# Feed-forward stages of a two-layer decoder: VectorE's and ScalarE's queues in the order of the text, with silu placed behind a weight cast

## The chip, the core and the metric

The kernel runs on one core of a Trainium2 chip. Times are device microseconds (us) of one execution. The median of three runs before the change is 2691.31 us (2690.03 to 2691.76). Engines are named as in the profile: PE is TensorE's matmul, PEld its weight load, DVE is VectorE, ACT is ScalarE, POOL is GpSimd, SP is SyncE, which here issues the loads of the weights.

## What is computed

Two decoder layers over 256 tokens of width 2048: first a dilated-window attention, then a latent attention, each followed by a SwiGLU feed-forward. The change touches the feed-forward stages alone:

```python
D_MODEL = 2048; SEQ = 256; FFN_HIDDEN = 5632

def swiglu(xn, w_gu, w_down):
    g, u = jnp.split(xn @ w_gu, 2, axis=-1)
    return (jax.nn.silu(g) * u) @ w_down

...
        h = h + swiglu(rms_norm(h, ffn_norm_g[layer]), ffn_w_gu[layer], ffn_w_down[layer])
    return rms_norm(h, final_norm_g)
```

All of it is float32. The kernel multiplies in a reduced format (fp32r) and splits every number into a high and a low half, so that one product becomes three matmuls: high by high, high by low, low by high.

## The kernel before, in words

**Weights.** All weight matrices stream through one `WeightStream`, in a fixed list of units, here called weight tiles: 128 partitions by 2048 floats, 1 MB. A weight tile is loaded by SP into one of three `raw` buffers (two DMAs of 512 KB in the feed-forward), then split: ACT casts it to the high half `hi` (line 167 for a whole tile, line 157 for half of one), DVE subtracts to get the low half `lo` (line 168 or 158). There are three buffers each for `hi` and `lo`. `ws.next()` (line 196) hands out the next tile, and before that splits the tile two ahead and issues loads three ahead of that (`more`, line 192). So while PE works on tile k, tile k+2 is being split, into the buffers that tile k-1 has just left.

**Two kinds of tile.** An "eight" tile takes 24 matmuls of 512 columns. A "seven" tile (`SEVEN`, tiles 2, 4 and 6 of a group) saves one of eight block products: `split_blocks` first makes sums of its blocks on DVE (lines 181 to 183, into `raw` and `sums`), casts and subtracts the tile (`hi`, `lo`) and the sums (`th`, `tl`, one buffer each), and takes 21 matmuls. For it the activations need sums as well (`sums`, from line 656: `f` in line 661, four `g` in line 666, then two casts and two subtracts, into x itself and into `forms` or `forms_h`).

**Groups.** `mixed` computes one group: 8 weight tiles against x, into two accumulators of two PSUM banks each, `la` and `ra`, plus four single banks for the "seven" tiles. After the last "seven" tile the four banks are folded into two SBUF tiles, `left` and `right` (line 724 on ACT, lines 725 to 727 on DVE). In the last tile of a group the 12 matmuls of `la` come first, then the 12 of `ra`. When `la` is done, `close(0, la)` is called, then `ws.more()`, which splits the next group's tile 1; when `ra` is done, `close(1, ra)`. There are only two accumulators, so the next group's first matmul needs `la` to be read out.

**A gate/up group.** 512 hidden columns of gate and up. `close` (from line 745) adds the accumulator to `gate` or `up` (line 748, DVE), then either silu of both token tiles (line 752, ACT) or the product of up and silu (line 754, DVE). Afterwards `turned` is put off by one tile (`later.put(1, turned)`): it runs behind the first tile of what follows, and transposes the result on PE (line 405, eight transposes), splits it into `hT` (line 380 on ACT, line 381 on DVE), and for the groups j = 4, 8 and 12 of the first two parts also makes sums of `hT`. In the first group of a layer there is no "seven" tile: silu reads `la` itself, and the scalings of x (`scaled`, line 674) and its sums are put off into this group and the next one.

**Parts.** The 44 hidden tiles of 128 go in parts of 16, 16 and 12 (`FFN_PARTS`): four, four and three gate/up groups, each part followed by its down product. The down product of the first two parts is two `mixed` groups whose `close` adds to the residual `h` (line 770), after which POOL adds the folded part by accumulating DMAs (line 774). The down product of the last part goes by `product` and adds in line 778. There are 11 gate/up groups in a layer, 22 in all.

**What sets the order.** The text is a plain list of operations; every wait is derived from what the operations read and write. The order in each engine's queue is set by a planner when the program is built: it goes through its own reckoning of time and may move an instruction of an engine ahead of others that stand before it in the text, as long as its data are ready. Each engine then issues its queue in that order.

Of the kernel before, what the change touches and what calls it, by code (L numbers as in the profile page):

```python
# [13 lines left out]
AF = mybir.ActivationFunctionType  # L14
ALU = mybir.AluOpType
# [4 lines left out]
NT = S // P  # L20
# [25 lines left out]


SEVEN = (2, 4, 6)
SEVEN_DOWN = {16: (2, 4, 6), 12: ()}


# [173 lines left out]
def kernel(ctx, tc, consts, x, attn_norm_g, ffn_norm_g, a_w_qkv, a_w_o, kv_norm_g,  # L225
                       b_w_kv_a, b_kv_a_norm_g, b_w_kv_b, b_w_q_a, b_q_a_norm_g, b_w_q_b, b_w_o,
                       ffn_w_gu, ffn_w_down, final_norm_g, out):
    nc = tc.nc
# [95 lines left out]
    def units_ffn(layer):  # L324
        for k0, n in FFN_PARTS:
            v = ffn_w_gu[layer].rearrange("(k p) c -> p k c", p=P)
            for j in range(k0, k0 + n, 4):
                for kp in range(KD // 2):
                    blocks = [v[:, 2 * kp:2 * kp + 2, b + j * P:b + j * P + 512] for b in (0, FF)]
                    units.append((blocks, None, "seven" if j > 0 and kp in SEVEN else "eight"))  # L330
            v = ffn_w_down[layer].rearrange("(k p) c -> p k c", p=P)
# [212 lines left out]
    with tc.tile_pool(name="attn_a", bufs=2) as ap:  # L544
# [45 lines left out]
        for quad in range(HEADS // 4):  # L590
            vs = []
            for g in range(NG):
                acc = product(x_stationary, xT, KD)
# [4 lines left out]
            for pair in range(2):  # L598
                st = {}
                for g in range(NG):  # L600
                    qk = []
                    for which in range(2):
                        acc = product(w_stationary, xT, KD, cols=(col(0), col(1)))
                        t = ap.tile([P, 2, S], F32, tag=f"qk{which}", name=f"qk{which}")
# [34 lines left out]

    def ffn(xT, rstd, finish):  # L640

        with tc.tile_pool(name="ffn", bufs=1) as fp:
            ws.sum_pool = fp

            r2, rem = [small.tile([P, NT], F32, tag=m, name=m) for m in ("r2", "rem")]
# [5 lines left out]
            later.put(1, lambda: row.update(R=across(r2, "R")))  # L651
            forms = fp.tile([P, len(SEVEN), 2, 3, P], F32R, name="forms")

# [16 lines left out]
            def scaled(kp):  # L670
# [4 lines left out]
                if kp in SEVEN:  # L675
                    sums(xT, kp, forms[:, SEVEN.index(kp)])

            def mixed(X, pairs, seven, sums_of, left, right, close):

                la, ra = acc_tile(), acc_tile()
                pb, begun = None, set()

                def first(m):
                    new = m not in begun
                    begun.add(m)
                    return new

                def mul(out, x, w, i, st, sp):
                    (xh, xl), (wh, wl) = x, [t[:, i * 512:(i + 1) * 512] for t in w]
                    mm(out=out, lhsT=xh, rhs=wh, start=st, stop=False)  # L693
                    mm(out=out, lhsT=xh, rhs=wl, start=False, stop=False)  # L694
                    mm(out=out, lhsT=xl, rhs=wh, start=False, stop=sp)  # L695

                for kp in range(pairs):
                    ends = kp == pairs - 1
                    w = ws.next(late=ends)
                    x = lambda t, kk: [X[:, 2 * kp + kk, o + t * P:o + (t + 1) * P] for o in (0, S)]  # L700
                    if kp in seven:
                        i = seven.index(kp)
                        st, sp = i == 0, i == len(seven) - 1
                        if st:
                            pb = [bank() for _ in range(4)]
                        y = lambda j: x(1, 0) if j == 0 else [sums_of[:, i, h, j - 1, :] for h in range(2)]
                        mul(pb[0], x(0, 0), w[:2], 1, st, sp)
                        mul(la[:, 0], x(0, 1), w[:2], 3, first("la0"), False)
                        mul(pb[1], y(0), w[:2], 0, st, sp)
                        mul(ra[:, 0], y(3), w[:2], 2, first("ra0"), False)  # L710
                        mul(pb[3], y(2), w[2:], 0, st, sp)
                        mul(pb[2], y(1), w[2:], 1, st, sp)
                        mul(la[:, 1], x(1, 1), w[2:], 2, first("la1"), False)
                    else:
                        for i, (acc, m) in enumerate(((la, "la"), (ra, "ra"))):
                            for t in range(NT):
                                mul(acc[:, t], x(t, 0), w, 1 - i, first(f"{m}{t}"), False)
                                mul(acc[:, t], x(t, 1), w, 3 - i, False, ends)
                            if ends and i == 0:
                                close(0, la)  # L720
                                ws.more()
                    later.tick()
                    if seven and kp == seven[-1]:
                        nc.scalar.copy(out=left[:, 0], in_=pb[0])
                        nc.vector.tensor_tensor(out=left[:, 1], in0=pb[2], in1=left[:, 0], op=ALU.add)
                        nc.vector.tensor_tensor(out=left[:, 2], in0=pb[3], in1=left[:, 1], op=ALU.add)
                        nc.vector.tensor_tensor(out=right, in0=pb[1].unsqueeze(1).broadcast_to([P, NT, 512]),
                                                in1=left[:, 1:3], op=ALU.subtract)
                close(1, ra)
# [4 lines left out]
            for part, (k0, n) in enumerate(FFN_PARTS):  # L734
                last = part == len(FFN_PARTS) - 1
                hT = big_tile([P, 16, 2 * S], F32R, "hT")
                for j in range(0, n, 4):
                    gate, up = pair_tiles()
                    first = k0 + j == 0
                    if first:  # L740
                        for kp in range(KD // 2):
                            later.put(kp + 3, lambda kp=kp: scaled(kp))
                    sc_ = rstd if first else rem

                    def close(i, acc, first=first, both=(gate[:, 0:3:2], up), sc_=sc_):
                        d = both[i]
                        if not first:
                            nc.vector.tensor_tensor(out=d, in0=acc, in1=d, op=ALU.add)  # L748
                            acc = d
                        for t in range(NT):  # L750
                            if i == 0:
                                nc.scalar.activation(out=d[:, t], in_=acc[:, t], func=AF.Silu, scale=sc_[:, t:t + 1])
                            else:
                                nc.vector.scalar_tensor_tensor(out=d[:, t], in0=acc[:, t], scalar=sc_[:, t:t + 1],
                                                               in1=both[0][:, t], op0=ALU.mult, op1=ALU.mult)

                    def turned(j=j, up=up, hT=hT, seven=SEVEN_DOWN[n]):
                        transposed([up[:, t, :] for t in range(NT)], hT, j, None)
                        for kp in (j // 2, j // 2 + 1):
                            if kp in seven:  # L760
                                sums(hT, kp, forms_h[:, seven.index(kp)])
                    mixed(xT, KD // 2, () if first else SEVEN, forms, gate, up, close)
                    later.put(1, turned)

                for c in range(0, 0 if last else 4, 2):
                    left, right = pair_tiles()

                    def close(i, acc, c=c):
                        d = h[:, :, (c + i) * 512:(c + i + 1) * 512]
                        nc.vector.tensor_tensor(out=d, in0=acc, in1=d, op=ALU.add)  # L770

                    mixed(hT, n // 2, SEVEN_DOWN[n], forms_h, left, right, close)
                    for i, part_sum in enumerate((left[:, 0:3:2], right)):
                        nc.gpsimd.dma_start(out=h[:, :, (c + i) * 512:(c + i + 1) * 512], in_=part_sum,
                                            accum_op=ALU.add)

                def add(acc, c, t):
                    nc.vector.tensor_tensor(out=chunk(t, c), in0=acc[:, t, :], in1=chunk(t, c), op=ALU.add)
                    finish(c, t)

                for c in range(0 if last else 4, 4):
                    if ws.remaining() > n // 4:
                        acc = product(x_stationary, hT, n)
                        for t in range(NT):
                            add(acc, c, t)
                    else:
                        accs = [acc_tile() for _ in range(NT)]
                        tiles = [ws.next() for _ in range(n // 4)]
                        for t in range(NT):
                            for i, (hi, lo) in enumerate(tiles):  # L790
                                x_stationary(accs[t], hi, lo, hT, 4 * i, i == 0, i == len(tiles) - 1, ts=(t,))
                            add(accs[t], c, t)
# [23 lines left out]
    with tc.tile_pool(name="attn_b", bufs=2) as bp:  # L816
# [33 lines left out]
        acc = product(w_stationary, xT, KD, cols=(col(0),))  # L850
# [5 lines left out]
        scale = QH ** -0.5  # L856
# [32 lines left out]
        for hp in range(HEADS // 2):  # L889
            hi, lo = ws.next()  # L890
            acc = acc_tile()
# [11 lines left out]
            acc = acc_tile()  # L903
# [82 lines left out]
```

## Time and profile before

| | us |
|---|---|
| median of 3 runs | 2691.31 |
| lowest and highest | 2690.03, 2691.76 |
| the profiled execution | 2692.26 |
| its span in the trace | 2690.5 |
| PE busy in the span | 2654.1 (99%) |
| DVE busy | 2015.6 (75%) |
| ACT busy | 1291.8 (48%) |
| feed-forward of layer 0 | about 977 to 1697 |
| feed-forward of layer 1 | about 1962 to 2690 |

A row of a timeline reads: start in us from the span's start, length in us, engine, line of the kernel, operation, what it writes <- what it reads, shapes, how many were merged into the row, and, in brackets, idle time of the engine before it and what ended it. A row of the waits reads: who waited, for whom, total us, times, longest us. Matmuls overlap: each lasts 0.39 us in the trace, and the next one starts 0.23 after it.

### The profile page before, as it was taken

The page shows a single profiled execution, that of the slowest core. Times are in us where ns is not written, and L with a number is a line of the kernel's source. Part 1 is how long each engine was busy: PE and PEld are TensorE (multiplying, and loading weights), DVE is VectorE, ACT ScalarE, POOL GpSimd, SP SyncE. Part 2 cuts the span into 40 slices and gives each one's busy share as a digit, 9 for nine tenths or more (in the row PEclk, how much of TensorE's full clock was granted, in tenths as well). Part 3 has the DMA queues.
Part 4 walks back from the last instruction along what each step waited for, and adds up shares of the span by engine and source line. Part 5 has one row for each costly group of instructions (what it writes and reads, how often), then busy time and mean ns, then how long its engine had stood idle before and what let it go on. Part 6 is the DMA issues. An engine that isn't in the chain of part 4 may idle for free.

```text
span 2690.5 us, 32489 instructions
## 1 busy us (share of the span) xinstructions
PE 2654.1 (99%) x12914; PEld 2224.4 (83%) x12914; DVE 2015.6 (75%) x2458; ACT 1291.8 (48%) x1425; POOL 24.9 (1%) x28
## 2 busy tenths in 40 slices
PE   9999999999999999999999999999999999999998
PEld 7888888888888887888788888888878788878887
DVE  5676576476477668888988886588578888898884
ACT  5444444443434445554545454565445554454543
POOL 0000000000000000000000000000000000000000
PEclk9999999999999999999999999999999999999999
DMA  7545555555554555567566656444555576657663
GB/s 264 188 161 169 188 172 170 185 170 166 172 187 159 201 188 185 198 202 220 181 207 208 211 190 200 154 149 138 178 182 193 183 219 205 203 178 234 197 212 132
DMA packets 308089, 504.18 MB, mean 187 GB/s; under 512 B 13960, under 2 KB 117088, under 8 KB 307552
## 3 DMA queue, kind: packets, MB, share of 16 engines
q1 hardware_dynamic: 302960, 492.64, 55.3%
q0 software_dynamic: 4352, 8.39, 1.7%
q8 instruction: 101, 1.65, 0.2%
q10 hardware_dynamic: 624, 1.07, 0.1%
q14 instruction: 52, 0.43, 0.0%
HBM read 491.57 MB, written 2.10 MB: 183 GB/s over the span
## 4 chain that ended last, share of the span: by engine, by line
PE 90%; DVE 5%; issue 3%; ACT 2%; DMA 0%; SPq 0%; POOL 0%; POOLq 0%; DVEq 0%; ACTq 0%
PE acc L450 14%; PE acc L693 11%; PE acc L694 11%; PE acc L695 11%; PE acc L470 8%; PE acc L471 8%; PE acc L469 8%; PE acc L453 7%; PE bank L695 2%; PE bank L693 2%; PE bank L694 2%; DVE lo L168 2%; ACT hi L167 1%; PE bank L405 1%; PE bank L565 1%
## 5 line engine op out<-in xcount | busy, mean ns | idle before, releaser
L158 DVE TENSOR_TENSOR lo<-raw,hi 128x1024 fp32r<-128x1024 f32 (+2 forms) x450 | 515.8, 1167 | 349.6 <-ACT hi L157 333.7
L167 ACT CAST hi<-raw 128x2048 fp32r<-128x2048 f32 x240 | 459.2, 1913 | 597.3 <-PE acc L695 420.8
L157 ACT CAST hi<-raw 128x1024 fp32r<-128x1024 f32 (+2 forms) x450 | 432.6, 1006 | 555.2 <-PE acc L450 303.4
L168 DVE TENSOR_TENSOR lo<-raw,hi 128x2048 fp32r<-128x2048 f32 x240 | 548.1, 2288 | 153.5 <-ACT hi L167 153.2
L693 PE MATMUL acc<-hi,xT_f 128*128 128x512 f32 x988 | 389.4, 394 | 17.7 <-DVE gate L748 14.4
L694 PE MATMUL acc<-lo,xT_f 128*128 128x512 f32 x988 | 386.2, 391 | 0.0
L695 PE MATMUL acc<-hi,xT_f 128*128 128x512 f32 x988 | 385.7, 390 | 0.0
L450 PE MATMUL acc<-xT_a,hi 128*128 128x512 f32 x1536 | 379.3, 395 | 0.0
L450 PEld LDWEIGHTS acc<-xT_a,hi 128*128 128x128 f32 x1536 | 281.6, 188 | 53.8
L693 PEld LDWEIGHTS acc<-hi,xT_f 128*128 128x128 f32 x988 | 185.8, 188 | 63.2 <-issue 19.9
L695 PEld LDWEIGHTS acc<-hi,xT_f 128*128 128x128 f32 x988 | 185.9, 188 | 40.0
L694 PEld LDWEIGHTS acc<-lo,xT_f 128*128 128x128 f32 x988 | 186.0, 188 | 38.6
L453 PEld LDWEIGHTS acc<-xT_a,lo 128*128 128x128 f32 x1536 | 196.9, 191 | 7.5
L453 PE MATMUL acc<-xT_a,lo 128*128 128x256 f32 x1536 | 199.2, 283 | 0.0
L470 PE MATMUL acc<-lo,xT_a 128*128 128x512 f32 x384 | 150.6, 392 | 0.8 <-DVE lo L158 0.8
L471 PE MATMUL acc<-hi,xT_a 128*128 128x512 f32 x384 | 150.9, 393 | 0.0
L469 PE MATMUL acc<-hi,xT_a 128*128 128x512 f32 x384 | 150.8, 393 | 0.0
L168 DVE TENSOR_TENSOR tl<-sums,th 128x1536 fp32r<-128x1536 f32 x84 | 147.2, 1752 | 0.0
L693 PE MATMUL acc<-hi,hT 128*128 128x512 f32 x344 | 134.9, 392 | 4.1 <-DVE gate L748 4.1
L167 ACT CAST th<-sums 128x1536 fp32r<-128x1536 f32 x84 | 124.7, 1485 | 28.2 <-DVE sums L183 19.1
L694 PE MATMUL acc<-lo,hT 128*128 128x512 f32 x344 | 134.3, 390 | 0.0
L695 PE MATMUL acc<-hi,hT 128*128 128x512 f32 x344 | 134.1, 390 | 0.0
(260 smaller groups left out, 4006.9 us busy)
## 6 DMA issues: line engine op xcount, KB each, us to landing
raw<-in_ffn_w_gu_dram SPq DMA_DIRECT2D x352, 512.0 KB, 4.5
raw<-in_a_w_qkv_dram SPq DMA_DIRECT2D x143, 1024.0 KB, 4.8
raw<-in_ffn_w_down_dram SPq DMA_DIRECT2D x128, 512.0 KB, 4.7
raw<-in_ffn_w_down_dram SPq DMA_DIRECT2D x24, 1024.0 KB, 5.1
raw<-in_a_w_o_dram SPq DMA_DIRECT2D x16, 1024.0 KB, 5.0
raw<-in_b_w_o_dram SPq DMA_DIRECT2D x16, 1024.0 KB, 5.0
raw<-in_b_w_kv_b_dram SPq DMA_DIRECT2D x8, 1024.0 KB, 5.1
raw<-in_b_w_q_b_dram SPq DMA_DIRECT2D x8, 768.0 KB, 4.5
```

Source lines behind the costliest of these rows:

```text
L157: nc.scalar.copy(out=h, in_=src)
L158: nc.vector.tensor_tensor(out=l, in0=src, in1=h.bitcast(F32), op=ALU.subtract)
L167: self.nc.scalar.copy(out=hi, in_=src)
L168: self.nc.vector.tensor_tensor(out=lo, in0=src, in1=hi.bitcast(F32), op=ALU.subtract)
L450: mm(out=acc[:, i, :], lhsT=sl(hi, kk), rhs=xT[:, k0 + kk, :], start=first and kk == 0, stop=False)
L453: mm(out=acc[:, i, 0:S], lhsT=sl(lo, kk), rhs=xT[:, k0 + kk, 0:S], start=False, stop=last and kk == nk - 1)
L469: mm(out=acc[:, t, :ncol], lhsT=xh, rhs=rhs(hi, kk), start=st, stop=False)
L470: mm(out=acc[:, t, :ncol], lhsT=xh, rhs=rhs(lo, kk), start=False, stop=False)
L471: mm(out=acc[:, t, :ncol], lhsT=xl, rhs=rhs(hi, kk), start=False, stop=sp)
L693: mm(out=out, lhsT=xh, rhs=wh, start=st, stop=False)
L694: mm(out=out, lhsT=xh, rhs=wl, start=False, stop=False)
L695: mm(out=out, lhsT=xl, rhs=wh, start=False, stop=sp)
```

## The change

The whole body of `ffn` is placed in a region in which DVE and ACT issue their instructions in the order of the text. PE, SP and POOL stay with the planner, and so does the order across engines and where the region's instructions fall among those outside it. In the text itself one thing moves: `close(0, la)` of a gate/up group no longer issues silu; it returns it as a function, and `mixed` calls it behind `ws.more()`, that is, behind the cast and the subtract of the next group's tile 1. The `close` of a down group returns nothing.

```diff
+ORDERED = {mybir.EngineType.DVE, mybir.EngineType.Activation}
...
-        with tc.tile_pool(name="ffn", bufs=1) as fp:
+        with tc.tile_pool(name="ffn", bufs=1) as fp, tc.manual_schedule(engines=ORDERED):
...
                             if ends and i == 0:
-                                close(0, la)
+                                then = close(0, la)
                                 ws.more()
+                                if then:
+                                    then()
...
                         if not first:
                             nc.vector.tensor_tensor(out=d, in0=acc, in1=d, op=ALU.add)
                             acc = d
+
+                        def silu():
+                            for t in range(NT):
+                                nc.scalar.activation(out=d[:, t], in_=acc[:, t], func=AF.Silu, scale=sc_[:, t:t + 1])
+                        if i == 0:
+                            return silu
                         for t in range(NT):
-                            if i == 0:
-                                nc.scalar.activation(out=d[:, t], in_=acc[:, t], func=AF.Silu, scale=sc_[:, t:t + 1])
-                            else:
-                                nc.vector.scalar_tensor_tensor(out=d[:, t], in0=acc[:, t], scalar=sc_[:, t:t + 1],
-                                                               in1=both[0][:, t], op0=ALU.mult, op1=ALU.mult)
+                            nc.vector.scalar_tensor_tensor(out=d[:, t], in0=acc[:, t], scalar=sc_[:, t:t + 1],
+                                                           in1=both[0][:, t], op0=ALU.mult, op1=ALU.mult)
```

## The prediction

> **What bounds the kernel now.** I read the busy time of the engines in a feed-forward stage first, then the waits of TensorE, then the timelines of PE, DVE and ACT around the end of one group. The stretch of layer 0 (columns: length, busy us of PE, PEld, DVE, ACT, POOL, then granted clock, DMA share, GB/s):
>
> ```profile
> 977.00:1697.00 720.00, 709.23 (x3160) 581.85 (x3159) 605.46 (x531) 363.05 (x295) 10.46 (x9) 1.00 0.62 199
> ```
>
> TensorE is busy for 709.23 of 720 us, so only its idle time can be won. DVE comes next with 605.46 (84%); it is close enough to full that its order matters. TensorE's waits over the whole span (total, times, longest):
>
> ```profile
> PE acc L693 <- DVE gate L748: 18.5, 18, 1.0
> PE acc L693 <- ACT gate L752: 3.3, 2, 1.8
> ```
>
> These two rows are the stake: 20 ends of groups at which the next group's first matmul waits for the accumulator `la`, 18 times for the add of line 748, twice (first group of each layer) for silu, which reads `la` itself. One of the 18 on PE (A is the group that ends, B the next, a digit its weight tile):
>
> ```profile
> 1106.43 0.39 PE L695 MATMUL acc<-hi,xT_f 128*128 128x512 f32 x1
> ...
> 1109.15 0.39 PE L695 MATMUL acc<-hi,xT_f 128*128 128x512 f32 x1
> 1110.57 0.47 PE L693 MATMUL acc<-hi,xT_f 128*128 128x512 f32 x1 [1.03 <-DVE gate L748]
> 1110.88 0.40 PE L694 MATMUL acc<-lo,xT_f 128*128 128x512 f32 x1
> ...
> 1116.93 0.48 PE L693 MATMUL acc<-hi,xT_f 128*128 128x512 f32 x1
> ...
> 1127.30 0.40 PE L693 MATMUL acc<-hi,xT_f 128*128 128x512 f32 x1
> ```
>
> `la` is complete at 1106.43 + 0.39 = 1106.82, `ra` at 1109.54, and twelve matmuls lie between 1106.43 and 1109.15: 0.227 us each. Without a wait B0 would start at 1109.38; it starts at 1110.57, 1.19 late, and the matmul after it comes 0.31 behind instead of 0.23. One such wait costs 1.19 + 0.08 = 1.27 us. Why the add is late stands in DVE's queue:
>
> ```profile
> 1104.08 2.28 DVE L168 TENSOR_TENSOR lo<-raw,hi 128x2048 fp32r<-128x2048 f32 x1
> 1106.27 0.68 DVE L726 TENSOR_TENSOR gate<-bank,gate 128x512 f32<-128x512 f32 x1
> 1106.87 0.68 DVE L181 TENSOR_TENSOR raw<-raw 128x512 f32<-128x512 f32 x1
> 1107.47 1.22 DVE L727 TENSOR_TENSOR up<-bank,gate 128x1024 f32<-128x1024 f32 x1
> 1108.61 0.68 DVE L182 TENSOR_TENSOR sums<-raw 128x512 f32<-128x512 f32 x1
> 1109.21 1.22 DVE L748 TENSOR_TENSOR gate<-acc,gate 128x1024 f32<-128x1024 f32 x1
> 1110.34 1.22 DVE L748 TENSOR_TENSOR up<-acc,up 128x1024 f32<-128x1024 f32 x1
> 1111.47 1.22 DVE L183 TENSOR_TENSOR sums<-raw,sums 128x1024 f32<-128x1024 f32 x1
> 1112.60 1.41 DVE L754 SCALAR_TENSOR_TENSOR up<-up,rem,gate 128x512 f32<-128x512 f32 x2
> 1113.93 2.29 DVE L168 TENSOR_TENSOR lo<-raw,hi 128x2048 fp32r<-128x2048 f32 x1
> 1116.13 1.75 DVE L168 TENSOR_TENSOR tl<-sums,th 128x1536 fp32r<-128x1536 f32 x1
> 1117.80 0.69 DVE L181 TENSOR_TENSOR raw<-raw 128x512 f32<-128x512 f32 x1
> 1118.76 1.29 DVE L381 TENSOR_TENSOR hT<-bank,hT 128x512 fp32r<-128x512 f32 x2 [0.28 <-ACT hT L380]
> 1119.97 0.68 DVE L661 TENSOR_TENSOR f<-hT 128x512 f32<-128x512 f32 x1
> 1120.57 2.28 DVE L168 TENSOR_TENSOR lo<-raw,hi 128x2048 fp32r<-128x2048 f32 x1
> 1122.77 0.48 DVE L666 TENSOR_TENSOR g<-f 128x128 f32<-128x128 f32 x2
> ...
> 1132.06 0.68 DVE L181 TENSOR_TENSOR raw<-raw 128x512 f32<-128x512 f32 x1
> 1132.78 0.69 DVE L182 TENSOR_TENSOR sums<-raw 128x512 f32<-128x512 f32 x1
> ```
>
> The queue has no gap: the subtract for B1 (1104.08) and two sums for B2 stand ahead of the add, which starts at 1109.21, 2.4 us after `la` was complete. Successive rows also give the pitch: an instruction that doesn't read the one before it starts 0.08 before that one ends; one that does waits it out (L181 to L182: 0.72). The rows of ACT that matter below:
>
> ```profile
> 1111.43 1.33 ACT L752 ACTIVATE gate<-gate,rem 128x512 f32<-128x512 f32 x2
> 1112.72 1.49 ACT L167 CAST th<-sums 128x1536 fp32r<-128x1536 f32 x1
> 1116.34 1.91 ACT L167 CAST hi<-raw 128x2048 fp32r<-128x2048 f32 x1 [2.13 <-PE acc L695]
> ...
> 1124.74 0.51 ACT L380 CAST forms_h<-g 128x384 fp32r<-128x384 f32 x1
> ```
>
> The cast at 1116.34 is B3's. It runs as soon as B0 gives its buffer back, 8.4 us ahead of the cast for the sums of the finished group (1124.74), though the text has it behind.
>
> **What the text order does at these ends, walked from the rows.** DVE's queue becomes: L725 to L727, gate add, lo(B1), up add, L754 twice, the sums of B2 (L181 to L183), lo(B2), tl(B2), L381 twice, then, for 12 of the 18 ends, the sums of the finished group (f, four g, small casts), and only then lo(B3). The 12 are counted in the loops: groups j = 4, 8, 12 of two parts in two layers; at the other 6 `turned` has no sums.
>
> Gain: L727 no longer waits behind lo(B1), and after 1104.08 L726 and L727 need 0.72 + 1.22, so they are done near 1106.0. The gate add starts with `la` complete, 1106.85, and ends at 1108.07; B0 starts unhindered at 1109.38. All 18 waits go. Moving silu costs nothing here: B1's cast is long done, silu's 1.33 ends near 1109.5, and its reader L754 comes at 1111.4.
>
> Cost: what stands behind in order. lo(B1) 1107.98; up add 1110.19 (`ra`, complete at 1109.54, is free at 1111.41; B0 wants it at 1109.38 + 12 x 0.227 = 1112.10, so 0.7 us of room); L754 from 1111.44; L181 1112.77, L182 1113.49, L183 1114.22. B2's cast waits for L181 and takes 1.91 to 1115.39; lo(B2) 1115.42, tl(B2) 1117.63, L381 1119.30 (its transposes follow B0 on PE, which ends near 1114.8, and its casts wait behind th(B2), 1.49 from 1115.47; both are done by 1118.0), f 1120.51, g from 1121.23 (0.32 where one reads the one before, else 0.20) to 1122.23. The 0.51 cast for the sums starts at 1122.26, and B3's cast, held behind it, at 1122.69, where it now runs at 1116.34. It ends at 1124.60, lo(B3) runs from 1124.63 to 1126.92.
>
> When does PE want lo(B3)? B1 starts 6.36 - 0.08 after B0, B3 another 10.37 later: 1126.03; its second matmul, the first to read lo, 1126.26. PE follows an end on DVE within 0.14 (the gate add ended at 1110.43, the matmul started at 1110.57); I take 0.05, as this matmul's weights are already loaded. It is then 0.71 late, and the one after it again 0.08: **a new wait of 0.79 at B3 on lo of line 168**, 12 times. B4 then doesn't add to it: L181 at 1126.84, cast to 1129.46, lo to 1131.78, wanted by B4 at 1126.03 + 0.79 + 24 x 0.227 = 1132.3. By B6 the queue has caught up (B7's lo is some 3 us early). Without sums B3's cast follows the transposes' casts at 1118.0, lo(B3) ends near 1122.8: no wait.
>
> The end of this walk is a chain of some 18 steps, so I give the new wait 0 to 1.9 us: below, a chain 0.8 shorter; above, each step 0.06 longer. I take 0.79, as each step has a row of its own.
>
> Loads: lo(B1) moves 3.9 us later and holds its raw buffer as long, so the load of B4 starts that much later on SP.
>
> ```profile
> raw<-in_ffn_w_gu_dram SPq DMA_DIRECT2D x352, 512.0 KB, 4.5
> ```
>
> Two such pieces make a tile: issued near 1110.3, in by 1119.3 even one after the other, wanted at 1126.84. Cost nothing; the cover is 7 us. POOL's accumulating DMAs follow the adds of line 770, which are not late. The end of a down group has neither L754 nor `turned`, has no wait now and gets none.
>
> **The first group of each layer** (two waits for silu, 3.3 us in all). In order, the scaling of the next x tile, its sums and their casts stand ahead of B1's cast, and table load and silu behind it. Now:
>
> ```profile
> 1019.96 1.28 ACT L752 ACT_TABLE_LOAD   x1
> 1021.25 1.27 ACT L752 ACTIVATE gate<-acc,rstd 128x512 f32<-128x512 f32 x2
> ```
>
> From the end of A5 the chain is B0's cast 1.91, lo 2.2, the scaling 1.25 (L674, of the form of L748), f 0.72, the g's 1.0, the casts of the sums 0.43, B1's cast 1.91, load 1.28, silu 1.27: 12.0 us against the 10.9 of 48 matmuls in A6 and A7, and some 0.2 for the handoffs. So silu ends about 1.3 late, where PE now waits 1.5 and up to 1.8; with the scalings of the last two x tiles in front, lo(B3) and lo(B4) come some 0.5 late each, by the same walk. Bounds: 3.3 us won if both waits go, as much lost if they double. I take 0, the value nearest to the walk.
>
> Two pages bear on this place. The Trainium skill, "ScalarE: Activation LUTs", section "What ACT_TABLE_LOAD costs", gives a load of about 1283 ns and a drain of about 1380 ns more; by it silu would come 1.38 later, 2.8 us in both layers, and the sum would be 2681. The trace agrees on the load (1.28) and not on the drain: silu starts 0.01 after it. In layer 1 the clock row behind the 1.8 us wait reads:
>
> ```profile
> 2009.00:2010.00 1.00, 1.00 (x4) 0.81 (x3) 1.00 (x2) 0.13 (x1) 0.00 (x0) 0.50 0.83 307
> ```
>
> The Trainium skill, "TensorE: Matmul & The Clock Gate", section "Part 1: The HAM clock gate (the "warmup" mystery)", has the clock halved after an idle window of about 3.4 us. Here it was 0.50 after a wait of half that, so the trace doesn't bear this bound out. By the page the drop would not hang on this wait and would stay; by the trace it may go with a shorter one. I keep it, so both give the same sum.
>
> **Sum.** 18 x 1.27 = 22.9 won, 12 x 0.79 = 9.5 given back: 13.4 us. The profiled execution took 2692.26 us (span 2690.5 and 1.8 around it), 0.95 above the median of the runs. 2692.26 - 13.4 - 0.95 = **2678**.
>
> **Rivals.**
> 1. No new wait: the chain is shorter, or the cast of B3 isn't held. For it: only 0.7 us decides. All of 22.9 stays: 2668.
> 2. The chain is longer by 0.5 us or more. DVE at 84% speaks for it. The new wait is then 1.3 to 1.9 and gives back 15.6 to 22.8: 2684 to 2691.
> 3. Slower: the planner, which still orders PE, puts the eight transposes of `turned` behind B1 instead of B0, because in its own reckoning L754 comes later. They then run at 1114.8 + 5.46 = 1120.3 at the earliest, the L381s at 1121.4, all behind them 2.1 us later than walked: B3 waits 2.9, 12 x (2.9 - 1.27) = 20 lost, 6 x 1.27 won: 12 us slower, 2703. It decides if L754's end passes B0's end; on my walk 1112.9 against 1114.8, and now, with 1114.0 against 1116.0, PE keeps them behind B0. So it is unlikely.
> 4. The change doesn't do what it says: the add of line 748 still starts late, because L726 and L727 end after 1106.85. There is 0.8 us of room. Then 2691.
>
> **How the numbers follow.** Forecast 0.56, rival 1 0.16, rival 2 0.12, rival 3 0.10, rival 4 0.06. What a measurement can tell here is about 0.2%, 5.4 us. Faster by more: the forecast, rival 1 and the quarter of rival 2 with a wait under 1.46, 0.75; within: the rest of 2 and rival 4, 0.15; slower: rival 3, 0.10. The range reaches from 2666, rival 1 with part of the first groups' waits gone as well, to 2690, most of rival 2, and leaves out rivals 3 and 4.
>
> **What would show it.** Right: the wait of PE on gate L748 gone from the list; the gate add starting within 0.1 us of the end of `la`; a new row, PE acc L694 waiting for DVE lo L168, near 12 times 0.7 us, after the groups with sums only; B3's cast behind the cast of forms_h. Wrong: that new row absent (rival 1) or well over 1 us (rival 2); transposes of `up` after B1 (rival 3); gate L748 still in the waits of PE (rival 4).

## The result and the profile after

The changed kernel takes 2678.86 us (median of 5 runs, 2678.4 to 2680.5); five runs of the kernel before taken with it have a median of 2691.76 (2690.03 to 2692.81). The ratio is 0.9954, with a 95% interval of 0.9939 to 0.9968: 12.9 us faster. The profiled execution took 2679.72, its span 2677.9. The line numbers have moved: 748 of before is 751 here, 752 is 756, 754 is 760, 167 and 168 are 168 and 169, 181 to 183 are 182 to 184, and 693 to 695 are 694 to 696.

The engines' busy time on the page of after:

```profile
PE 2652.6 (99%) x12914; PEld 2225.2 (83%) x12914; DVE 2039.7 (76%) x2458; ACT 1289.5 (48%) x1425; POOL 24.9 (1%) x28
```

The work of TensorE is the same within 1.5 us; what changed is its idle time. Its waits after (who for whom: total, times, longest):

```profile
PE acc L695 <- DVE lo L169: 7.9, 13, 1.0
PE acc L694 <- ACT gate L756: 2.7, 2, 1.4
```

The wait for the gate add, 18 times 1.0 before, is gone. A wait for `lo` stands in its place, and the two waits for silu have shrunk from 3.3 to 2.7. The end that the prediction walks, on VectorE:

```profile
1108.36 1.23 DVE L751 TENSOR_TENSOR gate<-acc,gate 128x1024 f32<-128x1024 f32 x1 [0.70 <-PE acc L696]
1109.50 2.28 DVE L169 TENSOR_TENSOR lo<-raw,hi 128x2048 fp32r<-128x2048 f32 x1
...
1117.06 2.29 DVE L169 TENSOR_TENSOR lo<-raw,hi 128x2048 fp32r<-128x2048 f32 x1
...
1124.45 0.56 DVE L382 TENSOR_TENSOR forms_h<-g,forms_h 128x384 fp32r<-128x384 f32 x1 [0.38 <-ACT forms_h L381]
1126.27 2.29 DVE L169 TENSOR_TENSOR lo<-raw,hi 128x2048 fp32r<-128x2048 f32 x1 [1.25 <-ACT hi L168]
```

The gate add now waits for PE, not PE for it: VectorE stood idle for 0.70 before it. The three subtracts are those of B1, B2 and B3. In front of the third VectorE is idle again, for 1.25, and ScalarE is the one that it waits for:

```profile
1109.67 1.34 ACT L756 ACTIVATE gate<-gate,rem 128x512 f32<-128x512 f32 x2 [3.32 <-DVE gate L751]
...
1123.91 0.51 ACT L381 CAST forms_h<-g 128x384 fp32r<-128x384 f32 x1 [0.38 <-DVE g L667]
1124.33 1.91 ACT L168 CAST hi<-raw 128x2048 fp32r<-128x2048 f32 x1
```

B3's cast (1124.33) starts directly behind the cast for the sums (1123.91); ScalarE does nothing but wait for those sums meanwhile. TensorE at the same place:

```profile
1107.93 0.39 PE L696 MATMUL acc<-hi,xT_f 128*128 128x512 f32 x1
...
1110.87 0.39 PE L694 MATMUL acc<-hi,xT_f 128*128 128x512 f32 x1
...
1128.61 0.51 PE L695 MATMUL acc<-lo,xT_f 128*128 128x512 f32 x1 [0.51 <-DVE lo L169]
1128.95 0.40 PE L696 MATMUL acc<-hi,xT_f 128*128 128x512 f32 x1
```

`la` is complete at 1107.93 + 0.39 = 1108.32 in this trace, the add starts 0.04 later, and B0 starts at 1110.87 without a wait. The matmul that reads B3's `lo` starts 0.05 after that subtract has ended (1126.27 + 2.29 = 1128.56).

### The profile page after: what moved, and what is told of

Same layout as the page of the kernel before. It is cut to its first block, busy times and chain, and to the rows that moved or that the text cites. A ratio compares the mean times of both kernels' runs of the same rounds, so it can differ in the third digit from the quotient of the medians.

```text
span 2677.9 us, 32417 instructions
## 1 busy us (share of the span) xinstructions
PE 2652.6 (99%) x12914; PEld 2225.2 (83%) x12914; DVE 2039.7 (76%) x2458; ACT 1289.5 (48%) x1425; POOL 24.9 (1%) x28
## 3 DMA queue, kind: packets, MB, share of 16 engines
q10 hardware_dynamic: 624, 1.07, 0.1%
## 5 line engine op out<-in xcount | busy, mean ns | idle before, releaser
L694 PE MATMUL acc<-hi,xT_f 128*128 128x512 f32 x988 | 385.5, 392 | 2.7 <-ACT gate L756 2.7
L694 PEld LDWEIGHTS acc<-hi,xT_f 128*128 128x128 f32 x988 | 185.6, 188 | 42.9 <-ACT gate L756 3.6
L694 PE MATMUL acc<-hi,hT 128*128 128x512 f32 x344 | 134.1, 392 | 0.0
```

## The experiments

The question was which of the three parts of the change (VectorE in order, ScalarE in order, silu moved) gives the gain and which gives some of it back. The theory: VectorE's order brings the gate add forward and is the whole gain; ScalarE's order, which holds B3's cast behind the casts of the sums, is the loss; silu's move does nothing by itself. Medians of the kernel before in these sessions were 2690.95, 2691.04 and 2690.91. Where an edit adds lines, the line numbers move again: L701, L760 and L767 below are L694, L751 and L756 of the changed kernel.

**The region without silu's move.**

```diff
                         if i == 0:
-                            return silu
+                            return silu()
```

> The region kept, silu issued again right behind the gate add and so ahead of the cast of the next group's tile 1. Theory (in-order queues decide, and each thing held pays at the next need): silu waits for the gate add, so B1's cast ends 6.5 us later than in the changed kernel, lo(B1) 3.4 us later, and the add of `up` behind lo(B1) as well; PE then waits about 2.9 us for `ra` in B0 at each of the 18 ends and about 1.1 us more for lo(B3) at the 12 ends with sums. 18 x (2.9 - 1.27) + 12 x 1.2 = 44 us slower than before: about 2735 us. Rival (ACT is busy for 48% only, so the place of silu in its queue does not matter and the order alone did it): 2679 us, the same as the changed kernel.

Measured: 2741.94 (2741.72 to 2742.07), ratio 1.019 (1.0176 to 1.0204): slower by 51. The waits of TensorE, and then ScalarE, VectorE and TensorE at the same end:

```profile
PE acc L695 <- DVE lo L169: 46.8, 34, 1.8
PE acc L694 <- ACT hi L168: 4.8, 12, 0.4
```

```profile
1114.73 1.34 ACT L756 ACTIVATE gate<-gate,rem 128x512 f32<-128x512 f32 x2 [6.45 <-DVE gate L751]
1115.98 1.90 ACT L168 CAST hi<-raw 128x2048 fp32r<-128x2048 f32 x1
```

```profile
1113.41 1.23 DVE L751 TENSOR_TENSOR gate<-acc,gate 128x1024 f32<-128x1024 f32 x1 [0.70 <-PE acc L696]
1117.90 2.29 DVE L169 TENSOR_TENSOR lo<-raw,hi 128x2048 fp32r<-128x2048 f32 x1 [3.26 <-ACT hi L168]
```

```profile
1118.65 0.39 PE L694 MATMUL acc<-hi,xT_f 128*128 128x512 f32 x1
1120.25 0.50 PE L695 MATMUL acc<-lo,xT_f 128*128 128x512 f32 x1 [1.21 <-DVE lo L169]
```

ScalarE is idle for 6.45 with B1's cast in its queue, because silu stands ahead and waits for the add. B1's `lo` ends at 1120.19, 6.8 us behind the start of the gate add; in the changed kernel it is 3.4 (1111.78 against 1108.36). The place of the wait is not where either theory had it. PE, which the planner still orders, takes the `la` part of B1 right after the 12 matmuls of B0's `la` (1118.65) and not after the whole of B0, and there it wants B1's `lo` (1120.25). The 34 waits are 20 of this kind, one at each end, and 14 on B3's `lo` (1.59 each) behind which the late queue had run up. So with the region, silu's place is worth 2741.94 - 2678.86 = 63 us.

**Silu's move without the region.**

```diff
-        with tc.tile_pool(name="ffn", bufs=1) as fp, tc.manual_schedule(engines=ORDERED):
+        with tc.tile_pool(name="ffn", bufs=1) as fp:
```

> Silu moved behind the cast in the text, no region: the planner orders all queues. Theory: the planner moves instructions by its own reckoning anyway, the gate add stays late, PE waits 18 times on it as before: 2691 us, within 3 us. Rival (the move of silu is what helped): near 2679 us, with the 18 waits gone.

Measured: 2691.29 (2689.59 to 2692.06, 11 runs), ratio 1.0001 (0.9992 to 1.0009). The waits are those of before:

```profile
PE acc L694 <- DVE gate L751: 18.5, 18, 1.0
PE acc L694 <- ACT gate L756: 3.3, 2, 1.8
```

The move changes nothing where the planner sets the order.

**The sums of the finished group one tile later.** The changed kernel; the transposes stay behind B0, the sums of `hT` come behind B1 and so behind B3's cast and subtract in the text.

```diff
                     def turned(j=j, up=up, hT=hT, seven=SEVEN_DOWN[n]):
                         transposed([up[:, t, :] for t in range(NT)], hT, j, None)
+                    def summed(j=j, hT=hT, seven=SEVEN_DOWN[n]):
                         for kp in (j // 2, j // 2 + 1):
...
                     later.put(1, turned)
+                    later.put(2, summed)
```

> The changed kernel with the sums of the finished group put off by one more tile, so that in the text they stand behind the split of B3 instead of ahead of it. Theory (B3's cast held behind the casts of the sums is the whole of the new wait): the 12 waits of PE on lo of B3 go, B4 has 1 us of room left: 12 x 0.79 = 9.5 us, and up to 1.5 more at the three ends that wait longer: 2668 to 2670 us. Rival (DVE has too much work at these ends, whatever the order): the wait moves to B4 or B5 and the time stays within 3 us of 2679.

Measured: 2668.05 (2667.4 to 2668.43), ratio 0.9916 (0.9902 to 0.9929). ScalarE, then VectorE, at the same end:

```profile
1116.79 1.93 ACT L168 CAST hi<-raw 128x2048 fp32r<-128x2048 f32 x1
1122.83 0.30 ACT L381 CAST hT<-g 128x128 fp32r<-128x128 f32 x1 [4.11 <-DVE g L667]
```

```profile
1119.53 2.28 DVE L169 TENSOR_TENSOR lo<-raw,hi 128x2048 fp32r<-128x2048 f32 x1
1121.73 0.68 DVE L662 TENSOR_TENSOR f<-hT 128x512 f32<-128x512 f32 x1
```

B3's cast and subtract run ahead of the sums, and the 12 waits on `lo` behind sums are gone. By the two ratios, (0.9954 - 0.9916) x 2691 = 10.2 us of the change's loss lay in the place of these sums, on both engines together.

**One engine of the region at a time.** First VectorE alone, then ScalarE alone:

```diff
-ORDERED = {mybir.EngineType.DVE, mybir.EngineType.Activation}
+ORDERED = {mybir.EngineType.DVE}
```

> The region for DVE alone; ACT is left to the planner, which may again run B3's cast ahead of the casts of the sums. Theory (it is ACT's order that holds B3's cast): on DVE lo(B3) still stands behind the sums, but starts 1.35 us earlier, as it need not wait for its cast; that is more than the 0.68 us by which PE waits: the 12 waits go, about 2668 us, as with the sums put later. Rival (DVE's own order holds lo(B3)): the 12 waits stay, 2679 us.

```diff
-ORDERED = {mybir.EngineType.DVE, mybir.EngineType.Activation}
+ORDERED = {mybir.EngineType.Activation}
```

> The region for ACT alone; DVE is left to the planner, as before the change. Theory (DVE's order makes the gain, ACT's order the loss): the gate add stays late, its 18 waits stay, and B3's cast is held behind the casts of the sums as in the changed kernel, which gives up to 2 us more at 12 ends: 2691 to 2715 us, not under 2690. Rival (ACT's order had a part in the gain): the waits on the gate add are gone or shorter, under 2685 us.

VectorE alone: 2673.4 (2672.56 to 2673.71), ratio 0.9934 (0.9922 to 0.9947), between the theory and its rival. Its waits, then ScalarE, VectorE and TensorE:

```profile
PE acc L695 <- DVE lo L169: 2.6, 11, 0.6
PE acc L694 <- DVE gate L751: 1.2, 3, 0.5
```

```profile
1118.08 1.93 ACT L168 CAST hi<-raw 128x2048 fp32r<-128x2048 f32 x1
```

```profile
1123.29 0.56 DVE L382 TENSOR_TENSOR forms_h<-g,forms_h 128x384 fp32r<-128x384 f32 x1 [0.38 <-ACT forms_h L381]
1123.76 2.29 DVE L169 TENSOR_TENSOR lo<-raw,hi 128x2048 fp32r<-128x2048 f32 x1
```

```profile
1126.10 0.50 PE L695 MATMUL acc<-lo,xT_f 128*128 128x512 f32 x1 [0.22 <-DVE lo L169]
```

B3's cast is early again, yet its subtract still stands behind the sums in VectorE's own order, and the matmul that reads it waits 0.22. The list of waits makes this look smaller than it is. Counted from start to start of the matmuls, the 12 ends with sums cost 0.43 to 0.84 each here, 6.1 in all, where they cost 10.8 in the changed kernel. So the theory that the loss is ScalarE's order alone doesn't hold: freeing ScalarE takes away 4.7 of the 10.8, and the rest stays with VectorE in order. Another part of this run's gain comes from a place that the expectation doesn't name: the two waits for silu in the first groups are gone, 3.3 by the same count, as ScalarE takes B1's cast ahead of the sums of x there (1016.18, where the changed kernel has it at 1019.23). Against that, the gate add starts late at ten ends and costs 3.2, at nine of them directly behind other work on VectorE; the three waits in the list are the longest of these.

ScalarE alone: 2687.22 (2686.07 to 2688.26, 11 runs), ratio 0.9987 (0.9978 to 0.9995). Its waits, then ScalarE at the end of the first group:

```profile
PE acc L694 <- DVE gate L751: 18.7, 18, 1.0
```

```profile
1019.38 1.28 ACT L756 ACT_TABLE_LOAD   x1 [0.80 <-PE acc L696]
1020.67 1.27 ACT L756 ACTIVATE gate<-acc,rstd 128x512 f32<-128x512 f32 x2
```

All 18 gate-add waits stay, and B3 shows no wait, though its cast is held behind the cast for the sums here too:

```profile
1121.12 0.51 ACT L381 CAST forms_h<-g 128x384 fp32r<-128x384 f32 x1 [0.85 <-DVE g L667]
1121.53 3.72 ACT L168 CAST hi<-raw 128x2048 fp32r<-128x2048 f32 x2
```

With VectorE left to the planner the sums are ready 2.8 earlier than in the changed kernel (1121.12 against 1123.91), and the cast comes in time. Both the theory and its rival missed by some 3 us: the 3.8 gained are the first groups' waits for silu and the stretch at half clock behind one of them (see the last section). Silu here starts ahead of the cast of B2's sums, on which neither had counted.

**The gate add alone.** No region; silu moved; the instructions of `ws.more()` behind `la`, and of the next group's first `ws.next()`, are queued behind the gate add on its engine, VectorE: the subtracts of B1 and B2 above all. All else is left to the planner.

```diff
+            added = []
+            def behind(pop):
+                if not added:
+                    return nullcontext()
+                return tc.issue_after(added.pop() if pop else added[-1])
...
-                    w = ws.next(late=ends)
+                    with behind(pop=True) if kp == 0 else nullcontext():
+                        w = ws.next(late=ends)
...
-                                ws.more()
+                                with behind(pop=False):
+                                    ws.more()
...
+                            if i == 0:
+                                added.append(ins.ins)
```

> No region. The planner orders all queues, silu is behind the cast as in the change, and one thing alone is fixed: on DVE the split of the next group's tiles 1 and 2 is queued behind the gate add. Theory (the late gate add is the whole of the 18 waits, and the planner keeps B3's cast ahead of the sums' casts): the 18 waits go and no new one comes, 18 x 1.27 = 22.9 us: about 2668 us, the same as with the sums put later. Rival (the text order of the rest is needed, or DVE has no room for the add this early): new waits on lo at tiles 1 to 4, 2675 us or more.

Measured: 2666.23 (2665.99 to 2667.83), ratio 0.9909 (0.9894 to 0.9924). The one wait of the feed-forward that is left, and VectorE at the same end:

```profile
PE acc L701 <- ACT gate L767: 3.3, 2, 1.8
```

```profile
1104.90 1.23 DVE L760 TENSOR_TENSOR gate<-acc,gate 128x1024 f32<-128x1024 f32 x1 [0.72 <-PE acc L703]
1106.04 2.28 DVE L169 TENSOR_TENSOR lo<-raw,hi 128x2048 fp32r<-128x2048 f32 x1
```

Putting this work behind one instruction per group gives 24.8 us, and no new wait comes.

**That kernel with ScalarE in order**, the suspected loss added to the bare gain:

```diff
-        with tc.tile_pool(name="ffn", bufs=1) as fp:
+        with tc.tile_pool(name="ffn", bufs=1) as fp, tc.manual_schedule(engines={mybir.EngineType.Activation}):
```

> The gate add fixed on DVE, the region for ACT alone. Theory (with ACT in text order the first group's silu stands ahead of the sums' cast of B2, as in the run with the region for ACT alone, which had no wait there; and the planner, which knows of ACT's order, places DVE's work so that no new wait comes): the 18 waits and the 2 of the first groups go: 2666.2 - 3.6 = about 2662.6 us. Rival (B3's cast held behind the casts of the sums makes PE wait again, now that B0 starts 1.27 us earlier): new waits at up to 12 ends, 2668 us or more.

Measured: 2714.65 (2711.97 to 2717.02), ratio 1.0088 (1.0074 to 1.0102). Its waits, then ScalarE at the same end:

```profile
PE acc L701 <- ACT hi L168: 16.5, 12, 1.4
PE bank L701 <- ACT hi L168: 12.8, 12, 1.1
```

```profile
1126.36 0.51 ACT L381 CAST forms_h<-g 128x384 fp32r<-128x384 f32 x1 [1.39 <-DVE g L667]
1126.78 3.70 ACT L168 CAST hi<-raw 128x2048 fp32r<-128x2048 f32 x2
```

The theory missed, and its rival had the direction but not the size. ScalarE's order costs 48 us here, against 5.5 in the change (2678.86 - 2673.4): the planner spreads the sums on VectorE among other work, and ScalarE in order waits them out with the casts of B3 and B4 behind. At exactly the 12 ends with sums PE waits twice for `hi`, 29 us in all, and some 13 go to a lower clock (granted on the mean 0.994, against 0.999 without ScalarE's order, over 2710 us).

**The silu waits of the first groups.** Three kernels load silu's table earlier. The first adds to the kernel with later sums a silu whose result nothing reads:

```diff
+            warm = small.tile([P, 1], F32, tag="warm", name="warm")
+            nc.scalar.activation(out=warm, in_=mhalf[:, 0:1], func=AF.Silu)
```

> The changed kernel with the sums one tile later, and one silu of a 128x1 column at the start of each feed-forward stage, so that the table is loaded there. Theory: the only wait left at the ends of the groups is that of the first group for silu, 1.36 us, and 1.28 of it is the load; both layers lose it: 2668.05 - 2 x 1.4 = about 2665 us. Rival (the load comes again ahead of the real silu, or silu waits for B1's cast anyway): 2668 us.

Measured: 2666.81 (2666.53 to 2667.32), ratio 0.991 (0.9896 to 0.9923), and the waits for silu as they were (two, 2.7 in all). The added silus do run, but not where the text has them:

```profile
2.48 0.29 ACT L652 ACTIVATE warm<-mhalf 128x1 f32<-128x1 f32 x2
```

What they read is ready from the start, and the planner put both at the start of the program. The attention then loads another table (L509, at 159.7), and silu's is loaded again directly ahead of the first real silu (1018.32), as before. So the attempt tells nothing of a load at the start of the stage, and the first of the next two expectations is mistaken where it says that this silu was dropped. In the next two a silu of `rstd`, scaled by zero, is added to `rem`: it depends on the stage's own data, so it can't move to the start of the program. The first is the kernel with later sums, the second the one with the gate add alone:

```diff
+            zero = small.tile([P, NT], F32, tag="zero", name="zero")
+            nc.scalar.activation(out=zero, in_=rstd, func=AF.Silu, scale=0.0)
...
+            nc.vector.tensor_tensor(out=rem, in0=rem, in1=zero, op=ALU.add)
```

> The changed kernel with the sums one tile later, and the silu table loaded at the start of each feed-forward stage by a silu of 128x2 numbers times zero, made of rstd and added to rem, so that it can neither be dropped nor moved to the start of the program (the silu of the run before was dropped: no row of the trace has it). Theory: 1.28 of the 1.36 us that PE waits for the first group's silu is the load; both layers lose 1.3 to 1.6: 2668.05 - 2 x 1.5 = 2665 us, and that wait is under 0.2 us. Rival (silu there waits for something else, such as B1's cast): the wait stays, 2668 us.

> No region, the gate add alone fixed on DVE, and the early table load. Theory: the first group's waits of 1.50 and 1.78 us are the load for 1.28 and the cast of B2's sums ahead of silu for the rest; with the load gone 0.2 to 0.5 us are left: 2666.2 - 2 x 1.3 = 2663.6 us, the fastest version. Rival (the planner puts other work on ACT into the place of the load): 2666 us.

With later sums: 2667.63 (2666.54 to 2668.47), ratio 0.9913 (0.9899 to 0.9926), no gain, against the theory. In the other: 2663.65 (2662.84 to 2665.58), ratio 0.99 (0.9886 to 0.9913), the fastest of all. The wait that the one has in the first groups, and the one that the other has:

```profile
PE acc L698 <- DVE lo L169: 2.6, 2, 1.3
```

```profile
PE acc L704 <- ACT gate L770: 0.4, 1, 0.4
```

In both the wait for silu is gone but for 0.4. In text order as much comes back at B3 of the same groups, where VectorE and ScalarE still have the scalings and sums of x ahead of B3's split; with the planner nothing comes back.

## Why the prediction was right

**18 gate-add waits at 1.27, 22.9 won: held.** The add starts 0.04 after `la`, and no such wait is left. The kernel with the gate add alone gained 24.8; its trace lacks the half-clock stretch of before (1.7, below), and what is left, 23.1, fits this term, if one trace of each stands for all executions.

**A new wait of 0.79 at B3, 12 times, 9.5 given back: held in place and cause, a little small.** The idle time of 0.51 at 1128.61 is the wait as the profile counts it; from start to start of the matmuls it is 0.68 more than the usual 0.23, and the matmul after it comes 0.34 behind instead of 0.23: 0.68 + 0.11 = 0.79. At 9 of the 12 ends it is this number. At the second group's end in each layer it is 1.17 + 0.11, at one more 1.03 + 0.11. Together 9 x 0.79 + 2 x 1.28 + 1.14 = 10.8, against 10.2 by the experiment with later sums. The second group's end shows why:

```profile
1063.58 1.22 DVE L730 TENSOR_TENSOR up<-bank,gate 128x1024 f32<-128x1024 f32 x1
1064.90 1.23 DVE L751 TENSOR_TENSOR gate<-acc,gate 128x1024 f32<-128x1024 f32 x1
...
1082.82 2.29 DVE L169 TENSOR_TENSOR lo<-raw,hi 128x2048 fp32r<-128x2048 f32 x1 [1.26 <-ACT hi L168]
```

From the gate add to B3's subtract it is 17.92 here and 17.91 at the end walked (1108.36 to 1126.27): the same chain. But the add itself comes without idle time before it, behind a full queue. PE wanted B3's `lo` at 1128.61 - 0.68 = 1127.93 there, 19.57 after the add; here at 1085.17 - 1.17 = 1084.00, 19.10 after it. So the add is 0.47 late, which is what rival 4 would have had in full, and that much is added to the wait. Where VectorE's backlog at this end comes from (the scalings of the first group are near) is argued only. Why one more end has 1.03 stays open.

**First groups: 0 was taken; about 0.5 net was won, out of parts that the walk had only in part.** The waits for silu shrank to 1.35 and 1.36 (the walk gave 1.3):

```profile
1021.15 1.28 ACT L756 ACT_TABLE_LOAD   x1
1022.45 1.26 ACT L756 ACTIVATE gate<-acc,rstd 128x512 f32<-128x512 f32 x2
```

```profile
1023.76 0.50 PE L694 MATMUL acc<-hi,xT_f 128*128 128x512 f32 x1 [1.35 <-ACT gate L756]
```

That is 0.6 won. The half-clock stretch behind the 1.78 wait of before lasted 3.4 us, half of it lost; it is gone, 1.7 won where the prediction had kept it. After each layer's first group PE waits for `lo` of B3, where the prediction had 0.5 each: 0.51 + 0.11 lost in layer 1 (the 13th wait of the list), 0.25 + 0.12 in layer 0; B4 shows no wait. And the walk missed one more cost: in the order of the text the instructions that make `R`, the row by which x is scaled, stand behind a subtract and four more on VectorE, and PE waits for them.

```profile
986.71 0.47 DVE L435 TENSOR_SCALAR R<-ident,r 128x128 f32<-128x128 f32 x2
```

Before, the same row stood at 981.75. PE now reaches the wait for silu 45.46 us behind the first matmul of the feed-forward, where it took 45.05 before; in layer 1 the two are 45.52 and 45.15. That is 0.8 lost. Together 0.6 + 1.7 - 1.0 - 0.8 = 0.5. Silu starts 0.02 after the table load has ended, so the 1.38 more, which the Trainium skill, "ScalarE: Activation LUTs", section "What ACT_TABLE_LOAD costs", gives for a drain, doesn't show here either.

**Silu's move costs nothing; the loads cost nothing: held.** Silu at 1109.67 ends at 1111.01, its reader starts at 1113.02. No wait of PE on a load of weights has come. B1's cast does wait for its load now (1.23, to 1104.45), but it is done at 1106.36, 3.1 ahead of its subtract.

**The sum.** 22.9 - 10.8 + 0.5 = 12.6. The two profiled executions differ by 2692.26 - 2679.72 = 12.5, but not by these terms alone. The changed kernel's execution is 0.9 behind when the feed-forward begins (its first matmul at 976.95, before at 976.02), ahead of the stages that were changed; some 0.8 the other way is spread over many small steps, and its cause is open. PE came to the first group's wait of layer 0 at 1022.57 - 1.50 = 1021.07 before,

```profile
1022.57 0.50 PE L693 MATMUL acc<-hi,xT_f 128*128 128x512 f32 x1 [1.50 <-ACT gate L752]
```

and at 1023.76 - 1.35 = 1022.41 after. So the mechanism of the forecast held, and that 2678 came within 1 us of the median (2678.86) is in part luck: 1.3 too little was given back at B3, 0.5 too little won in the first groups, where 1.7 won at the clock hid 1.8 lost elsewhere.

**The rivals.** Of rival 2 (a longer chain) the three ends above 0.8 are a part. Rival 3, the planner reordering PE, didn't come in the change, but it is no idle thought: with silu ahead of B1's cast the planner did reorder PE, by other instructions than the transposes, and that kernel lost 51. Rival 1's time, 2668, is what the two kernels reach in which neither B3's cast nor its subtract is held behind the sums, 2668.05 and 2666.23. Rival 4, the late gate add, came in part with VectorE alone in order.

## What to carry to other kernels

An engine's queue in the order of the text fixes one late instruction and makes a held one of every instruction that stands behind a wait in it; look in each engine's timeline for idle time ahead of an instruction whose data had long been there (here 1.25 on VectorE, for a cast that stood behind another's wait). If one instruction is late, putting only the competing work behind it was worth 24.8 us, against 12.9 for the order of two engines. Walk the queue to the end of the next group before believing a gain: what is late next stood 18 steps behind.

## What the runs showed of the hardware

TensorE's granted clock fell to half for a stretch after some short waits and not after others. In the kernel before it did after a wait of 1.78 us (the row of 0.50 in the prediction). The kernel with the gate add alone has the same wait at the same place, and the microsecond after it ran at full clock:

```profile
1994.74 0.50 PE L701 MATMUL acc<-hi,xT_f 128*128 128x512 f32 x1 [1.78 <-ACT gate L767]
```

```profile
1995.00:1996.00 1.00, 1.00 (x5) 0.79 (x5) 1.00 (x3) 1.00 (x1) 0.00 (x0) 1.00 1.01 387
```

The kernel with the region and silu unmoved shows six such stretches in the feed-forward, each 3.41 us long, some 10 of its 51 us, though it has fourteen waits of 1.59 or 1.60; the kernel with the gate add alone and ScalarE in order has eight, and twelve pairs of waits of 1.37 and 1.07. The Trainium skill, "TensorE: Matmul & The Clock Gate", section "Part 1: The HAM clock gate (the "warmup" mystery)", has the clock fall after an idle window of about 3.4 us; the length of the stretch is that of its window, while the waits here are half as long. What tells two equal waits apart can be read from the clock records of the traces. In each trace the starts of the half-clock stretches lie on one grid of 3.413 us, within 0.01: in the kernel before they are at 8.59, 2008.80 and, behind the last matmul, 2684.64, which is 586 and 198 steps apart. Add up TensorE's idle time in each step of the grid, in the feed-forward stages of all twelve traces. The 16 steps with the clock halved right behind them have 1.76 to 2.44 us of it, over half of the step; the steps with 1.63 or less are never followed by half clock (in the first microseconds of the kernel, among small matmuls, 1.43 by this count was enough). One step is an exception, that of the row above: it has 1.78, ends 0.16 behind the wait, and the clock stays full. So it counts how much of the waiting falls into one step, and the grid stands differently against the start of the kernel in each trace. The bound, between 1.63 and 1.78, is worked out from these traces and was not tested by a kernel made for it.
